# The first modulation chunk is requested between the x tiles, and ten modulation chunks move from the matrix to the vector engine

## The chip, the core and the metric

The kernel runs on one core of one Trainium2 chip. The metric is device time in microseconds (us) for one execution, taken as the median of three runs. In the rows, PE is TensorE's matrix products and PEld its weight loads, DVE is VectorE, ACT is ScalarE, POOL is GpSimd, and SP is the engine whose queue issues most of the loads from HBM.

## The reference

Two transformer blocks over 512 tokens of width 1024, in float32. The change concerns the modulation of the first block: six vectors of 1024 numbers, made by one matrix-vector product with a 1024 x 6144 matrix, which scale and shift the normed input ahead of the mixer (sh1, sc1) and ahead of the feed-forward part (sh2, sc2), and gate what each of the two adds to x (ga1, ga2).

```
c_act = jax.nn.silu(c)
mod = c_act @ ada_w[l] + ada_b[l]
sh1, sc1, ga1, sh2, sc2, ga2 = [m[:, None, :] for m in jnp.split(mod, 6, axis=-1)]
h = rmsnorm(x, pre_mix_g[l]) * (1.0 + sc1) + sh1
y = hybrid_mixer(h, ...)          # GLU projection, causal conv, stick-breaking attention, gates, merge, w_o
x = x + ga1 * rmsnorm(y, post_mix_g[l])
h = rmsnorm(x, pre_ffn_g[l]) * (1.0 + sc2) + sh2
y = swiglu_ffn(h, ...)
x = x + ga2 * rmsnorm(y, post_ffn_g[l])
# second block: retention, latent attention, conv feed-forward, final norm
```

## The kernel before

Every large product is made in three passes of 32-bit "round" numbers (`mm3`, L205 to L207): high part by high part, low by high, high by low. So each weight slab of 128 x 1024 passes through a fixed line: SP loads it into one of two buffers `w_st` (L186), ACT rounds it to `w_hi` (L187), DVE (or POOL) makes the rest `w_lo` (L210), and PE uses both; `w_hi` and `w_lo` have four buffers each. `ORDER` lists the slabs in order of use.

The stages are these. **Start:** the four x tiles (128 tokens each, 512 KB) are loaded, normed by `norm_of` (ACT squares and sums into `junk`, DVE adds a constant, POOL takes the power -0.5, DVE scales), then for each of eight blocks `kb` of 128 features `glu_in(kb)` gets modulation chunk kb, transposes the x tiles into `ps_t` and evacuates them as `hh`, `hf` (ACT) and `hl` (POOL); six GLU products follow. For kb = 0 the 512 tokens are done in two halves. **Attention:** the convolution taps run on DVE, ACT and POOL under the attention's products. **Merge:** for four pairs p, gates, the two branches' outputs and their sum. **wo and boundary:** the product with w_o, the residual, the next norm. **fin and fout:** the feed-forward part. Then the second block.

A modulation chunk (`ada_load`, `ada_acc`) is 1024 x 256 of the matrix: two loads `ad` of 512 KB and eight PE products of 32 columns x 256 (L373) which put four partial sums side by side in `ps_t`, one DVE copy to `acc` (L378), and a product with ones that sums over the partitions: `ada_cols` makes two columns from it (L384, for the scale and shift), `ga_row` a broadcast row (L404, for the gate). Of the 24 chunks eight are used at the start, six during the attention (`AD` sets where), six in the merge (two by `ada_cols`, four by `ga_row(0, ...)`), and four in the fin stage, at m = 4, 8, 12 and 16 (`fin_extra`).

The order on each engine is set when the program is built: a list scheduler with its own time estimates places the instructions; each engine then runs its list in order, and waits at the head of the list for what is not ready. SP's list is one queue, too: a load that waits for a free buffer holds all loads behind it.

Of the kernel before, what the change touches and what calls it, by code (L numbers as in the profile page):

```python
# [8 lines left out]
F32 = mybir.dt.float32  # L9
# [3 lines left out]
AF = mybir.ActivationFunctionType  # L13
ALU = mybir.AluOpType
# [6 lines left out]
NT = 4  # L21
# [69 lines left out]
AOFF = (0, 512, 896, 1152)  # L91
AGRP = ((0,), (1,), (2, 3))
NST = 2


def build(tc, nc, a):
    stacks = []

    def pool(name, bufs=1, side="left", **kw):
        s = ExitStack()  # L100
        p = s.enter_context(tc.tile_pool(name=name, bufs=bufs, side=side, reuse_waits="tile", **kw))
        stacks.append(s)
        return p, s

    def close(*ss):
        for s in ss:
            s.close()
# [6 lines left out]
    psT, _ = pool("psT", 2, space=PSUM)  # L114
    psP, _ = pool("psP", 4, space=PSUM)
    psC, _ = pool("psC", 2, space=PSUM)
    const, _ = pool("const")
    sm, _ = pool("small", 8)
    ring, _ = pool("ring")
    edge, _ = pool("edge", side="right")  # L120
    edge.tile([128, 96], F32, name="edge")
    hpool, _ = pool("hpool", side="right")

    def pt():
        ps_t = psT.tile([128, 512], F32, tag="t", name="ps_t")
        return ps_t
# [15 lines left out]
    vec = const.tile([128, NVEC], F32)  # L142
# [4 lines left out]
    ones = const.tile([128, 128], F32)  # L147
    mhalf = const.tile([128, 8], F32)
    eps1k = const.tile([128, 1], F32)
    zero = const.tile([128, 1], F32)  # L150
    halfpi = const.tile([128, 1], F32)
    cact = const.tile([128, 8, 32], F32)
    adab1 = const.tile([128, 48], F32)
    modA = const.tile([128, 2, 8], F32)
    modB = const.tile([128, 2, 8], F32)
    an32 = const.tile([128, 16], F32)
# [10 lines left out]
    def vcol(name, i):  # L167
        o = VOFF[name] + i
        return vec[:, o:o + 1]
# [8 lines left out]
    def emit_slab():  # L178
# [3 lines left out]
        n = src.shape[1]  # L182
        w_st = ring.tile([128, 1024], F32, tag="st", bufs=NST, name="w_st")
        w_hi = ring.tile([128, 1024], F32R, tag="hi", bufs=4, name="w_hi")
# [7 lines left out]
    def prefetch(n):  # L192
        while W.nxt < min(len(ORDER), W.got + n):
            emit_slab()
# [33 lines left out]
    def transposes(ps, srcs):  # L228
        for j, s in enumerate(srcs):
            r = s.shape[1]  # L230
            nc.tensor.transpose(out=ps[:r, j * 128:(j + 1) * 128], in_=s, identity=ident)  # L231
# [21 lines left out]
    def norm_of(x_t, jp, xn):  # L253
        r = rstd(sumsq(x_t, jp), None, eps1k)
        nc.vector.tensor_scalar(out=xn, in0=x_t, scalar1=r, scalar2=None, op0=ALU.mult)
# [98 lines left out]

    class ADA:
        pool, tag, bufs, nacc = ring, "st", NST, 1
        loaded = {}

    def ada_load(chunk):
        ads = []  # L360
        for hf in range(2):
            ad = ADA.pool.tile([128, 4, 256], F32, tag=ADA.tag, bufs=ADA.bufs, name="ad")
            nc.sync.dma_start(out=ad, in_=a["ada"][chunk][:, 4 * hf:4 * hf + 4, :])
            ads.append(ad)
        return ads

    def ada_acc(chunk, ap_):

        ads = ADA.loaded.pop(chunk, None) or ada_load(chunk)
        ps = pt()  # L370
        for hf, ad in enumerate(ads):
            for b in range(4):
                nc.tensor.matmul(  # L373
                    out=ps[32 * b:32 * b + 32, 0:256], lhsT=cact[:, 4 * hf + b, :], rhs=ad[:, b, :],
                    start=hf == 0, stop=hf == 1,
                )
        acc = ap_.tile([128, 256], F32, tag="acc", name="acc", bufs=ADA.nacc)
        nc.vector.tensor_copy(acc, ps[:, 0:256])  # L378
        return acc, ps[:, 256:512]

    def ada_cols(i, kb, g_name, ap_):
        acc, ps = ada_acc(8 * i + kb, ap_)
        for s in range(2):
            nc.tensor.matmul(  # L384
                out=ps[:, s:s + 1], lhsT=acc[:, s * 128:(s + 1) * 128], rhs=ones[:, 0:1], start=True, stop=True
            )
        sh, sc = 24 * i + kb, 24 * i + 8 + kb
        nc.vector.tensor_tensor(
            out=modB[:, i, kb:kb + 1], in0=ps[:, 0:1], in1=vcol("ada_b", sh), op=ALU.add
        )  # L390
        nc.vector.scalar_tensor_tensor(
            out=modA[:, i, kb:kb + 1], in0=ps[:, 1:2], scalar=adab1[:, sc:sc + 1], in1=vcol(g_name, kb),
            op0=ALU.add, op1=ALU.mult,
        )

# [18 lines left out]
    nc.vector.memset(eps1k, D * EPS)  # L414
    nc.vector.memset(zero, 0.0)
    nc.vector.memset(halfpi, float(np.float32(np.pi / 2)))

    endp, endp_s = pool("endp")
    cacc = endp.tile([128, 4, S], F32, tag="cacc", bufs=1)
# [4 lines left out]
    adp, adp_s = pool("ada", 2, side="right")  # L424
    xs = xin.tile([128, NT, D], F32)
    pos = const.tile([128, NT], I32)
    ADA.pool, ADA.tag, ADA.bufs, ADA.nacc = adp, "ad", 6, 2
    for tt in range(NT):
        nc.sync.dma_start(out=xs[:, tt, :], in_=a["x"][tt * 128:(tt + 1) * 128, :])
    ADA.loaded[0] = ada_load(0)  # L430
    nc.gpsimd.dma_start(out=cst, in_=a["const"])
    masks = adp.tile([128, 256], F32, tag="masks", name="masks", bufs=1)
# [4 lines left out]
    for _n in ("pre_mix_g", "pre_ffn_g"):  # L437
        _o = VOFF[_n]
        nc.vector.tensor_scalar(
            out=vec[:, _o:_o + 8], in0=vec[:, _o:_o + 8], scalar1=32.0, scalar2=None, op0=ALU.mult  # L440
        )
    _o = VOFF["ada_b"]
    nc.vector.tensor_scalar(out=adab1, in0=vec[:, _o:_o + 48], scalar1=1.0, scalar2=None, op0=ALU.add)
    nc.vector.tensor_copy(identb, ident)
    nc.vector.tensor_copy(strictb, masks[:, 0:128])
    nc.vector.tensor_copy(causalb, masks[:, 128:256])
    _o = VOFF["attn_norm_w_2"]
    nc.vector.tensor_scalar(out=an32, in0=vec[:, _o:_o + 16], scalar1=32.0, scalar2=None, op0=ALU.mult)
    _o = VOFF["mla_q_norm_w_2"]
    nc.vector.tensor_scalar(  # L450
        out=lat[:, 0:2], in0=vec[:, _o:_o + 2], scalar1=float(np.float32(16.0 * 96.0 ** -0.5)), scalar2=None,
        op0=ALU.mult,
    )
    nc.vector.tensor_scalar(
        out=lat[:, 2:3], in0=vec[:, _o + 2:_o + 3], scalar1=float(np.float32(np.sqrt(128.0))), scalar2=None,
        op0=ALU.mult,
    )

    for tt in range(NT):
        norm_of(xs[:, tt, :], adp, xs[:, tt, :])  # L460


    glu_ps = [pp() for _ in range(6)]

    def glu_in(kb, halves=1):
        ada_cols(0, kb, "pre_mix_g", adp)
        n = S // halves
        for i in range(halves):
            ps = pt()
            tts = range(i * NT // halves, (i + 1) * NT // halves)  # L470
            transposes(ps, [xs[:, tt, kb * 128:(kb + 1) * 128] for tt in tts])
            evac_h(ps[:, :n], kb, i * n, n, modA[:, 0, kb:kb + 1], modB[:, 0, kb:kb + 1], adp, True)

    glu_in(0, 2)
    for kb in range(KB):
        wh, wl = slab(("glu", kb))
        if kb < KB - 1:
# [2 lines left out]
        for t0 in range(0, S, n):  # L480
            for j in range(6):
# [3 lines left out]
                )  # L485
    ADA.pool, ADA.tag, ADA.bufs, ADA.nacc = ring, "st", NST, 1
    close(adp_s, xin_s)
# [312 lines left out]
    split_o(3)  # L800
    mtmp, mt_s = pool("mtmp", 4)
    grow_p, _gs = pool("growp", side="right")
    ADA.pool, ADA.tag, ADA.bufs = mtmp, "ad", 2
    grow1 = grow_p.tile([128, D], F32)
    for p in range(4):
        if p >= 2:
# [17 lines left out]
        for q in ((0,), (1, 2), (3,), ())[p]:  # L824
            ga_row(0, grow1, accp, q, mtmp)
    ADA.pool, ADA.tag, ADA.bufs = ring, "st", NST
    close(mt_s, endp_s)
# [161 lines left out]
    for tt, banks in gemm_tok([("c2", i) for i in range(4)], h_operand, 416, 4, seg=2):  # L989
        b = banks[tt, 0]  # L990
# [20 lines left out]
    for kb in range(3):  # L1011
        ps = pt()
        transposes(ps, [cT[:, tt, kb * 128:(kb + 1) * 128] for tt in range(NT)])
        sc = lat[:, kb:kb + 1]
        nc.scalar.activation(out=cTh[:, kb, :], in_=ps, func=AF.Identity, scale=sc)
        nc.vector.scalar_tensor_tensor(
            out=cTl[:, kb, :], in0=ps, scalar=sc, in1=cTh[:, kb, :].bitcast(F32), op0=ALU.mult, op1=ALU.subtract
# [218 lines left out]
    for b in range(2):  # L1236
        _, o = halves_of(b)
# [185 lines left out]
```

## Time and profile before

| | |
|---|---|
| median of 3 runs | 1425.65 us (1425.45 to 1426.05) |
| the profiled execution | 1426.3 us, span 1424.6 us |
| PE busy | 1378.3 us (97% of the span) |
| DVE busy | 731.9 us (51%) |
| ACT busy | 582.1 us (41%) |
| POOL busy | 325.1 us (23%) |
| mean granted TensorE clock | 0.991 |

The span runs from the first to the last instruction; the 1.7 us around it belong to the execution and not to the program's instructions. Busy shares are means over stages: what a stage is worth has to be read in that stage.

### The profile page before, as it was taken

The numbers are of one execution on the slowest core, as the hardware profiler recorded it, in microseconds if no ns is written. First come the engines' busy times: TensorE is split into PE (matmuls) and PEld (weight loads), VectorE is DVE, ScalarE is ACT, GpSimd is POOL, SyncE is SP. The second block draws the span as 40 slices with busy tenths as digits, with TensorE's granted clock in tenths as the row PEclk, the third lists the DMA queues.
The fourth block names the chain that finished last, engine by engine and source line by source line (L and its number), as shares of the span: only waits on it lengthen the run. The fifth ranks groups of instructions, "written<-read, shape, count | busy, mean of one in ns | idle before, by whom it ended". The sixth has DMA issues, their size and how long they took to land. (4 is left out here: it accounts for less than half of the span.)

```text
span 1424.6 us, 17617 instructions
## 1 busy us (share of the span) xinstructions
PE 1378.3 (97%) x6846; PEld 1119.7 (79%) x6846; DVE 731.9 (51%) x1132; ACT 582.1 (41%) x953; POOL 325.1 (23%) x329
## 2 busy tenths in 40 slices
PE   6999999999989999999999899999999999999998
PEld 4786777877878888888887788787888888888886
DVE  3299868254365332232333754688256655554334
ACT  4457655322244222222223525668345333333222
POOL 2189745321150000000002533377220000000000
PEclk9998999999999999999999999999999999999999
DMA  9422133564323344333232322001233323232321
GB/s 332 139 83 81 58 103 108 170 201 146 133 68 118 126 126 132 112 104 104 89 104 79 126 95 89 30 16 60 83 110 104 101 92 104 89 104 89 104 90 73
DMA packets 44324, 152.20 MB, mean 107 GB/s; under 512 B 4881, under 2 KB 7057, under 8 KB 44241
## 3 DMA queue, kind: packets, MB, share of 16 engines
q1 hardware_dynamic: 42720, 145.90, 31.0%
q0 software_dynamic: 1376, 4.97, 0.9%
q8 instruction: 54, 0.88, 0.3%
q14 instruction: 30, 0.24, 0.1%
q10 hardware_dynamic: 144, 0.21, 0.0%
HBM read 146.86 MB, written 4.19 MB: 106 GB/s over the span
## 5 line engine op out<-in xcount | busy, mean ns | idle before, releaser
L187 ACT CAST w_hi<-w_st 128x1024 fp32r<-128x1024 f32 (+2 forms) x217 | 225.3, 1039 | 395.6 <-PE ps_p L206 125.9
L210 DVE TENSOR_TENSOR w_lo<-w_st,w_hi 128x1024 fp32r<-128x1024 f32 (+2 forms) x179 | 222.4, 1244 | 258.5 <-ACT w_hi L187 256.6
L205 PE MATMUL ps_p<-hh,w_hi 128*128 128x512 f32 (+1 forms) x740 | 278.0, 382 | 1.9 <-ACT hh L266 1.2
L206 PE MATMUL ps_p<-hl,w_hi 128*128 128x512 f32 (+1 forms) x740 | 279.1, 378 | 0.4 <-POOL hl L210 0.4
L207 PE MATMUL ps_p<-hh,w_lo 128*128 128x512 f32 (+1 forms) x740 | 277.9, 376 | 1.4 <-DVE w_lo L210 1.4
L242 POOL TENSOR_TENSOR r<-q,mhalf 128x1 f32<-128x1 f32 x36 | 21.4, 595 | 768.4 <-DVE q L238 723.9
L205 PEld LDWEIGHTS ps_p<-hh,w_hi 128*128 128x128 f32 x740 | 139.4, 190 | 30.8 <-ACT hh L266 2.5
L207 PEld LDWEIGHTS ps_p<-hh,w_lo 128*128 128x128 f32 x740 | 140.4, 190 | 27.7 <-DVE w_lo L210 2.5
L206 PEld LDWEIGHTS ps_p<-hl,w_hi 128*128 128x128 f32 x740 | 140.6, 190 | 26.0 <-POOL hl L210 1.6
L205 PE MATMUL ps_c<-hh,w_hi 128*128 128x512 f32 (+1 forms) x354 | 130.4, 368 | 3.1 <-ACT hh L266 2.0
L206 PE MATMUL ps_c<-hl,w_hi 128*128 128x512 f32 (+1 forms) x354 | 130.0, 368 | 1.1 <-POOL hl L210 1.1
L207 PE MATMUL ps_c<-hh,w_lo 128*128 128x512 f32 (+1 forms) x354 | 128.6, 363 | 0.0
L210 POOL TENSOR_TENSOR w_lo<-w_st,w_hi 128x1024 fp32r<-128x1024 f32 (+1 forms) x38 | 93.1, 2455 | 67.0 <-ACT w_hi L187 47.1
L210 DVE TENSOR_TENSOR gl<-gf,gh 128x512 fp32r<-128x512 f32 x44 | 30.4, 690 | 105.6 <-ACT gh L869 105.5
L869 ACT CAST gh<-gf 128x512 fp32r<-128x512 f32 x44 | 27.4, 622 | 135.1 <-PE ps_p L206 124.1
L205 PEld LDWEIGHTS ps_c<-hh,w_hi 128*128 128x128 f32 x354 | 67.3, 190 | 15.9 <-ACT hh L266 2.5
L206 PEld LDWEIGHTS ps_c<-hl,w_hi 128*128 128x128 f32 x354 | 66.9, 189 | 11.7 <-POOL hl L210 1.3
L207 PEld LDWEIGHTS ps_c<-hh,w_lo 128*128 128x128 f32 x354 | 67.1, 189 | 11.0 <-issue 0.8
L207 PE MATMUL ps_p<-w_hi,gl 128*128 128x512 f32 x176 | 68.5, 389 | 0.0
L206 PE MATMUL ps_p<-w_lo,gh 128*128 128x512 f32 x176 | 68.5, 389 | 0.0
L205 PE MATMUL ps_p<-w_hi,gh 128*128 128x512 f32 x176 | 68.5, 389 | 0.0
L510 DVE SCALAR_TENSOR_TENSOR ps_c<-upad,vec,ps_c 128x512 f32<-128x512 f32 x87 | 60.6, 747 | 0.7
(423 smaller groups left out, 2536.0 us busy)
## 6 DMA issues: line engine op xcount, KB each, us to landing
ad<-in_ada SPq DMA_DIRECT2D x48, 512.0 KB, 4.0
w_st<-in_w_fin SPq DMA_DIRECT2D x44, 512.0 KB, 3.7
w_st<-in_w_up SPq DMA_DIRECT2D x44, 512.0 KB, 3.7
w_st<-in_w_win SPq DMA_DIRECT2D x22, 512.0 KB, 3.7
w_st<-in_w_fout SPq DMA_DIRECT2D x22, 512.0 KB, 3.6
w_st<-in_w_down SPq DMA_DIRECT2D x22, 512.0 KB, 3.7
w_st<-in_w_gate SPq DMA_DIRECT2D x16, 512.0 KB, 3.7
w_st<-in_w_wo SPq DMA_DIRECT2D x16, 512.0 KB, 3.7
```

Source lines behind the costliest of these rows:

```text
L187: nc.scalar.copy(w_hi[:, :n], w_st[:, :n])
L205: nc.tensor.matmul(out=out, lhsT=lh, rhs=rh, start=start, stop=False)
L206: nc.tensor.matmul(out=out, lhsT=lh, rhs=rl, start=False, stop=False)
L207: nc.tensor.matmul(out=out, lhsT=ll, rhs=rh, start=False, stop=stop)
L210: (eng or nc.vector).tensor_tensor(out=out, in0=src, in1=hi.bitcast(F32), op=ALU.subtract)
L242: nc.gpsimd.tensor_tensor(out=r, in0=q, in1=mhalf[:, 0:1], op=ALU.pow)
L510: nc.vector.scalar_tensor_tensor(out=out, in0=src, scalar=w, in1=acc, op0=ALU.mult, op1=ALU.add)
L869: nc.scalar.copy(gh, gf[:, k, :])
```

## The change

The change has four parts. (1) The start: only x tiles 0 and 1 are requested ahead of modulation chunk 0; then comes the first GLU slab (`prefetch(1)`), and only then x tiles 2 and 3, which are normed between the two halves of `glu_in(0)`. (2) A one-element silu at the very start makes ACT load the silu table first. (3) Twelve products of the ones tile by itself are put at the head of PE's list; nothing reads them. (4) From the merge on (`ADA.vector = True`, never reset, so in the fin stage too) a chunk's eight partial products are made on DVE: one multiplication and seven multiply-adds over 128 x 256, in place of eight PE products and the copy. The `1 + bias` table is made in place. No result differs but for the order of summation.

```
+    warm = sm.tile([128, 1], F32, tag="q", name="warm")
+    nc.scalar.activation(out=warm, in_=zero, func=AF.Silu)
+    idle = pt()
+    for _ in range(WARM):                                  # WARM = 12
+        nc.tensor.matmul(out=idle[:, 0:128], lhsT=ones, rhs=ones, start=True, stop=True)
...
-    for tt in range(NT):
-        nc.sync.dma_start(out=xs[:, tt, :], in_=a["x"][tt * 128:(tt + 1) * 128, :])
+    def load_x(tts):
+        for tt in tts:
+            nc.sync.dma_start(out=xs[:, tt, :], in_=a["x"][tt * 128:(tt + 1) * 128, :])
+
+    load_x((0, 1))
     ADA.loaded[0] = ada_load(0)
...
-    for tt in range(NT):
-        norm_of(xs[:, tt, :], adp, xs[:, tt, :])
...
-    def glu_in(kb, halves=1):
+    def glu_in(kb, halves=1, late=()):
         ada_cols(0, kb, "pre_mix_g", adp)
         n = S // halves
         for i in range(halves):
+            if i:
+                for tt in late:
+                    norm_of(xs[:, tt, :], adp, xs[:, tt, :])
...
-    glu_in(0, 2)
+    for tt in (0, 1):
+        norm_of(xs[:, tt, :], adp, xs[:, tt, :])
+    prefetch(1)
+    load_x((2, 3))
+    glu_in(0, 2, (2, 3))
...
     def ada_acc(chunk, ap_):
         ads = ADA.loaded.pop(chunk, None) or ada_load(chunk)
+        if ADA.vector:
+            acc = ap_.tile([128, 256], F32, tag="acc", name="acc", bufs=ADA.nacc)
+            for hf, ad in enumerate(ads):
+                for b in range(4):
+                    cc = cact[:, 4 * hf + b, 0:1]
+                    if hf == 0 and b == 0:
+                        nc.vector.tensor_scalar(out=acc, in0=ad[:, b, :], scalar1=cc, scalar2=None, op0=ALU.mult)
+                    else:
+                        nc.vector.scalar_tensor_tensor(
+                            out=acc, in0=ad[:, b, :], scalar=cc, in1=acc, op0=ALU.mult, op1=ALU.add
+                        )
+            return acc, pt()[:, 256:512]
...
-    ADA.pool, ADA.tag, ADA.bufs = mtmp, "ad", 2
+    ADA.pool, ADA.tag, ADA.bufs, ADA.vector = mtmp, "ad", 2, True
```

The list of ACT at the start shows what a late x tile stands behind; `-` is before, `+` is the change, `junk,ss` is the square sum of one x tile, `cact` the silu of c, and `w_hi` the rounding of a GLU slab.

```order
 L250 ACTIVATE junk,ss<-xs 128x1024
-L436 ACT_TABLE_LOAD
-L436 ACTIVATE cact<-vec 128x8
-L250 ACTIVATE junk,ss<-xs 128x1024 x3
-L187 CAST w_hi<-w_st 128x768 x2
+L459 ACTIVATE cact<-vec 128x8
+L250 ACTIVATE junk,ss<-xs 128x1024
+L187 CAST w_hi<-w_st 128x768
 L266 ACTIVATE hh<-ps_t,modB,modA 128x256
 L269 ACTIVATE hf<-ps_t,modB,modA 128x256
+L250 ACTIVATE junk,ss<-xs 128x1024 x2
+L187 CAST w_hi<-w_st 128x768
```

The table load between the first two square sums is gone; the square sums of x tiles 2 and 3, and the second slab's rounding, move behind the first half's `hh` and `hf`. On DVE the part that follows reads so in the changed kernel, from modulation chunk 0 on (`acc` to `modA`), with the two late tiles' `q` and `xs` between the slabs' `w_lo`:

```order
L393 COPY acc<-ps_t 128x256
L403 TENSOR_TENSOR modB<-ps_t,vec 128x1
L406 SCALAR_TENSOR_TENSOR modA<-ps_t,vec 128x1
L210 TENSOR_TENSOR w_lo<-w_st,w_hi 128x768
L236 TENSOR_TENSOR q<-ss,eps1k 128x1
L255 TENSOR_SCALAR xs<-xs,r 128x1024
L236 TENSOR_TENSOR q<-ss,eps1k 128x1
L210 TENSOR_TENSOR w_lo<-w_st,w_hi 128x768
L255 TENSOR_SCALAR xs<-xs,r 128x1024
```

Before, all four tiles' `q` and `xs` stood ahead of `acc`; now the last tile's scaling stands behind the second slab's `w_lo`, which itself needs ACT's rounding of that slab.

In the merge, DVE's list before has one copy for a chunk between the slabs' `w_lo`, the products with the gates (`gat`) and the merged operand's low part (`ml_`):

```order
L817 TENSOR_TENSOR gat<-gat,ps_c 128x512
L210 TENSOR_TENSOR ml__2669<-st,mh 128x512
L378 COPY acc<-ps_t 128x256
L210 TENSOR_TENSOR w_lo<-w_st,w_hi 128x1024
L210 TENSOR_TENSOR ml__2669<-st,mh 128x512
```

The changed list there, from the first of the merge's chunks on:

```order
L379 TENSOR_SCALAR acc<-ad,cact 128x256
L381 SCALAR_TENSOR_TENSOR acc<-ad,cact,acc 128x256 x7
L210 TENSOR_TENSOR w_lo<-w_st,w_hi 128x1024
L775 TENSOR_TENSOR st<-st,ps_c 128x512
L775 TENSOR_TENSOR st<-st,ps_p 128x512
L210 TENSOR_TENSOR w_lo<-w_st,w_hi 128x1024
```

A chunk is now eight instructions ahead of a `w_lo`; later chunks are cut into pieces of one to four between the other work. Behind the merge, at the boundary, ACT's list before, from the square sums of token tile 1's product on:

```order
L250 ACTIVATE junk,ss<-ps_c 128x512
L250 ACTIVATE junk,ss<-ps_p 128x512
L250 ACTIVATE junk,ss<-x_3168 128x1024
L187 CAST w_hi<-w_st 128x1024
L250 ACTIVATE junk,ss<-ps_p 128x512
```

and in the changed kernel:

```order
L250 ACTIVATE junk,ss<-ps_c 128x512
L250 ACTIVATE junk,ss<-ps_p 128x512
L187 CAST w_hi<-w_st 128x1024 x2
L250 ACTIVATE junk,ss<-x_3177 128x1024
L250 ACTIVATE junk,ss<-ps_p 128x512
```

Two slabs' roundings now stand ahead of the square sum of the new x of tile 1.

## Rows read from the trace of the kernel before

**Rows 1.** Stages: us, busy us (count) of PE, PEld, DVE, ACT, POOL, clock, DMA, GB/s.

```profile
11.89:14.03 2.14, 2.14 (x18) 0.69 (x18) 1.06 (x3) 0.00 (x1) 0.54 (x1) 1.00 1.03 416
287.00:362.00 75.00, 75.00 (x389) 55.32 (x388) 36.71 (x52) 18.60 (x24) 11.52 (x8) 1.00 0.53 177
399.00:431.00 32.00, 27.33 (x201) 24.90 (x200) 21.18 (x33) 15.58 (x31) 18.11 (x22) 0.95 0.24 75
431.00:600.00 169.00, 168.17 (x794) 136.39 (x793) 61.07 (x86) 47.70 (x58) 0.19 (x1) 1.00 0.38 123
```

**Rows 2.** PE's longest wait: us in total, times, longest us.

```profile
PE ps_t L373 <- DMA ad<-in_ada: 11.9, 1, 11.9
```

**Rows 3.** Timeline of PE at the start: start us, length us, instruction.

```profile
13.52 1.08 PE L373 MATMUL ps_t<-ad,cact 128*32 128x256 f32 x8
...
17.20 0.80 PE L205 MATMUL ps_p<-hh,w_hi 128*128 128x256 f32 x2
17.79 0.41 PE L205 MATMUL ps_c<-hh,w_hi 128*128 128x256 f32 x1
18.00 0.63 PE L205 MATMUL ps_p<-hh,w_hi 128*128 128x256 f32 x2
...
20.09 0.28 PE L207 MATMUL ps_p<-hh,w_lo 128*128 128x256 f32 x1
20.21 0.28 PE L206 MATMUL ps_p<-hl,w_hi 128*128 128x256 f32 x1
...
26.28 0.73 PE L205 MATMUL ps_p<-hh,w_hi 128*128 128x512 f32 x2
```

**Rows 4.** Timeline of ACT, DVE and POOL at the start.

```profile
9.99 1.06 ACT L250 ACTIVATE junk<-xs 128x1024 bf16<-128x1024 f32 x1
...
12.86 0.75 DVE L255 TENSOR_SCALAR xs<-xs,r 128x1024 f32<-128x1024 f32 x1 [0.66 <-POOL r L242]
...
14.03 1.81 ACT L187 CAST w_hi<-w_st 128x768 fp32r<-128x768 f32 x2 [2.89 <-DMA w_st<-in_w_glu]
...
15.01 0.95 DVE L210 TENSOR_TENSOR w_lo<-w_st,w_hi 128x768 fp32r<-128x768 f32 x1
...
17.04 0.56 ACT L269 ACTIVATE hf<-ps_t,modB,modA 128x256 f32<-128x256 f32 x1
...
17.68 0.73 POOL L210 TENSOR_TENSOR hl<-hf,hh 128x256 fp32r<-128x256 f32 x1 [4.85 <-ACT hf L269]
```

**Rows 5.** Timeline of PE in the merge, around half a chunk.

```profile
323.92 0.40 PE L205 MATMUL ps_p<-oh,w_hi 128*128 128x512 f32 x1
...
325.38 0.40 PE L205 MATMUL ps_p<-oh,w_hi 128*128 128x512 f32 x1
...
326.07 0.39 PE L205 MATMUL ps_p<-oh,w_hi 128*128 128x512 f32 x1
```

**Rows 6.** Timeline of PE in the fin stage, around a whole chunk.

```profile
501.97 0.39 PE L207 MATMUL ps_c<-hh,w_lo 128*128 128x512 f32 x1
...
503.29 0.50 PE L205 MATMUL ps_p<-hh,w_hi 128*128 128x512 f32 x1
```

**Rows 7.** Groups of DVE in the merge, by line and shape: busy, mean ns, idle before.

```profile
L210 DVE TENSOR_TENSOR w_lo<-w_st,w_hi 128x1024 fp32r<-128x1024 f32 x11 | 15.6, 1415 | 6.6 <-ACT w_hi L187 6.5
...
L406 DVE SCALAR_TENSOR_TENSOR grow<-grow,gr 128x256 f32<-128x256 f32 x4 | 1.7, 420 | 0.0
```

**Rows 8.** Timeline of DVE: one `w_lo` beside POOL, three chained multiply-adds.

```profile
331.39 2.27 DVE L210 TENSOR_TENSOR w_lo<-w_st,w_hi 128x1024 fp32r<-128x1024 f32 x1 [0.17 <-ACT w_hi L187]
...
452.46 0.94 DVE L909 SCALAR_TENSOR_TENSOR angles<-angles 128x128 f32<-128x128 f32 x3
```

**Rows 9.** DMA issues in the merge: count, KB each, median us to landing.

```profile
w_st<-in_w_gate SPq DMA_DIRECT2D x3, 512.0 KB, 5.4
```

**Rows 10.** Timeline of ACT and DVE at the boundary.

```profile
397.94 1.04 ACT L187 CAST w_hi<-w_st 128x1024 fp32r<-128x1024 f32 x1
...
399.56 2.35 DVE L210 TENSOR_TENSOR w_lo<-w_st,w_hi 128x1024 fp32r<-128x1024 f32 x2
```

More of the change, by code (lines that the diff above doesn't have):

```diff
@@ L93 @@
 NST = 2
+WARM = 12
 def build(tc, nc, a):
@@ L120, in build @@
     edge, _ = pool("edge", side="right")
-    edge.tile([128, 96], F32, name="edge")
+    edge.tile([128, 16], F32, name="edge")
     hpool, _ = pool("hpool", side="right")
@@ L152, in build @@
     cact = const.tile([128, 8, 32], F32)
-    adab1 = const.tile([128, 48], F32)
     modA = const.tile([128, 2, 8], F32)
@@ L356, in build @@
         pool, tag, bufs, nacc = ring, "st", NST, 1
-        loaded = {}
+        loaded, vector = {}, False
     def ada_load(chunk):
@@ L391, in ada_cols @@
         nc.vector.scalar_tensor_tensor(
-            out=modA[:, i, kb:kb + 1], in0=ps[:, 1:2], scalar=adab1[:, sc:sc + 1], in1=vcol(g_name, kb),
+            out=modA[:, i, kb:kb + 1], in0=ps[:, 1:2], scalar=vcol("ada_b", sc), in1=vcol(g_name, kb),
             op0=ALU.add, op1=ALU.mult,
@@ L442, in build @@
     _o = VOFF["ada_b"]
-    nc.vector.tensor_scalar(out=adab1, in0=vec[:, _o:_o + 48], scalar1=1.0, scalar2=None, op0=ALU.add)
+    for _i in (_o + 8, _o + 32):
+        nc.vector.tensor_scalar(
+            out=vec[:, _i:_i + 8], in0=vec[:, _i:_i + 8], scalar1=1.0, scalar2=None, op0=ALU.add
+        )
     nc.vector.tensor_copy(identb, ident)
```

## The prediction

> **What bounds the kernel now.** I read the stages first, then PE's waits, then the places that the change touches. In the merge, 287 to 362 us, PE is busy for all 75.00 us, and in the fin stage, 431 to 600, for 168.17 of 169 [rows 1]: what leaves PE's list there shortens the kernel, as long as nothing new is late. DVE is busy for 36.71 of the merge's 75 us and 61.07 of fin's 169 [rows 1], so it has room for more, on the mean. The boundary between the product with w_o and fin, 399 to 431, is different: PE is idle there for 4.67 of 32 us, and a chain over ACT, DVE and POOL sets the end [rows 1]. At the start PE waits 11.9 us, by far its longest wait, for modulation chunk 0 [rows 2]. The DMA engines are full by then (share 1.03, 416 GB/s, [rows 1]), so the order of the requests sets when that chunk lands.
>
> **The start.** The second half of chunk 0 is used at 13.52, and the first GLU product runs at 17.20, 3.68 us later [rows 3]. Two x tiles of 512 KB no longer lie ahead of the chunk: 1.05 MB at 416 GB/s is 2.5 us, so its second half should be used at about 11.0. The chain of 3.68 us stays, or gets a little shorter: I put the first GLU product at 14.4, 2.8 us earlier. But the second half of the tokens gets later. ACT has the square sums of x tiles 2 and 3 behind the first half's `hf`, which starts 0.16 before and ends 0.40 after that product [rows 3, 4], so at 14.8. Then come, one after the other: two square sums at 1.06 plus about 0.1 each, to 17.1; the second slab's rounding, 0.9 (half of the 1.81 for two), to 18.0; its `w_lo` on DVE, 0.95, to 19.0; the scaling of tile 3 behind it, 0.75, to 19.75 [rows 4]. Transposes and `hh` take about 0.6, as 16.6 to 17.2 before; the products of the second half start at 20.3. Their low part waits for `hf` and for `hl` on POOL (0.73, [rows 4]), to 21.5; twelve products at 0.12 (20.09 to 20.21, [rows 3]) make 22.95, and a whole chunk's products about 1.0 (1.09 in fin, worked out below), so that block 1 starts at 24.0, not at 26.28 [rows 3]: **-2.3 us**. From there on the blocks follow each other on PE as before. The bounds: nothing is gained if the late tiles take all of it (0 us), and the 2.8 us of the first half plus what a faster clock gives (next paragraph) make 4 us at most.
>
> The table load that goes was on ACT ahead of tile 1's square sum, under the wait for the chunk: nothing. The twelve idle products lie in the same wait of 11.9 us [rows 2]. No row shows one of them; by the nearest, a 128-column transposing product, they take a few us. If they took more than the 9.4 us to the new landing (11.9 - 2.5) they would delay the chunk, which they should not: the trace counts two passes for a float32 product (x8 for the four of half a chunk, [rows 3]), and 24 passes of 128 columns, each at the slow price of 256 (0.21, from 17.79 to 18.00, [rows 3]), are 5.0 us. What they may give is the clock. [...] At the faster level the chunk's products and the sums over partitions, some 1 us each in the chain, lose up to 0.5 us each; I take none of it, since the late tiles' chain on ACT and DVE sets block 1 anyway.
> [...]
>
> **The chunks that leave PE.** In the merge a half chunk stands between two products: L205 to L205 takes 1.46 us with it (323.92 to 325.38) and 0.69 without (325.38 to 326.07), so it costs 0.77 [rows 5]. In fin a whole chunk in one piece costs 503.29 - 501.97 - 0.23 = 1.09 [rows 6], 0.23 being a third of 0.69. Six chunks go from the merge, one of them in one piece there and five cut in halves: 1.1 + 10 x 0.77 = **-8.8 us**. Four go from fin, all in one piece: 4 x 1.09 = **-4.4 us**. The products with ones that follow a chunk stay.
>
> **What DVE takes on.** A multiply-add of 128 x 256 takes 0.420 us (L406, [rows 7]); chained ones start 0.03 further apart than they are long (three of 128 columns in 0.94, [rows 8]), so eight make at most 8 x 0.45 = 3.6 us. In the merge that is 6 x 3.6 = 21.6 on top of 36.7: 58.3 of the 66.2 that are left of the stage, 88%. In fin it is 14.4 on top of 61.1, of 165: hidden by DVE's idle half. In the merge the cover is thin. The instructions queued behind a chunk on DVE are the slabs' `w_lo`, `gat` and `ml_`; PE waits for `w_lo`. A slab takes 5.4 us from request to landing [rows 9], 1.05 to round, 1.2 to 2.3 for `w_lo` [rows 7, 8], some 8 to 9 us in all; two buffers make one slab per 4 to 4.5 us, and PE uses one up in 24 x 0.23 = 5.5. So each pair of slabs has 2 to 3 us to spare, and a chunk per pair takes 3.6 when it lies wholly ahead of a `w_lo`, as the first one does, and less where it is cut. Bounds: 0, when all of it falls into DVE's idle time, and 6 x 1.6 = 9.6 when no chunk is cut. DVE's list cuts five of six, so I take a value near the lower end, **+1.5 us**.
> [...]
>
> **The boundary.** ACT's list now has two roundings ahead of tile 1's square sum, and DVE two `w_lo` ahead of its norm: 2 x 1.04 = 2.1 us later, with 2.35 more on DVE 4.4 [rows 10], while PE waits for `hh`. On the other side the first slabs are ready earlier, and tile 3's chain, which sets the second half of the tokens, has less ahead of it. Bounds -2 (under half of PE's idle 4.67) and +4.4; I take **+1.0**. The second block's list is also reshuffled in its attention part, with the same work: 0, within 2 us either way.
>
> **The sum,** against the profiled execution: 1426.3 - 2.3 - 8.8 - 4.4 + 1.5 + 1.0 = 1413.3. That execution lay 0.65 above the median of the runs, so the median should come to 1412.6.
>
> **Rivals.** (A) DVE becomes the bound of the merge: each chunk holds a `w_lo` up and the merge keeps its length. Speaking for it: 88% of the stage, and POOL's 11.52 us there [rows 1], beside which a `w_lo` is up to 0.86 us longer (2.27 against 1.415, [rows 7, 8]); if all of POOL's time were added, DVE would need 69.8 us of the 66.2 left. Against it: the cut chunks and the four `w_hi`/`w_lo` pairs. Then the -8.8 and the +1.5 go: 1413.3 + 7.3 - 0.65 = 1420.0.
> (B) The start and the boundary go well: the late tiles are not late (-4 in place of -2.3), no new wait in the merge, the boundary gains 2: 1412.6 - 1.7 - 1.5 - 3.0 = 1406.4.
> (C) Slower: a chunk's first multiplication waits at the head of DVE's list for `ad` to land, 5.4 us after a request that SP may itself hold back, and everything behind it waits too. With ten chunks the gain of 15.5 is gone from 1.55 us of PE's time each; the full 5.4 each would give 1426.3 - 15.5 + 54 - 0.65 = 1464, a more likely 2.5 each 1435. Against it: two half-chunk buffers, each free after four instructions, and about 11 us between chunks.
> (D) The change does nothing measurable: the waits of (C) at about 1.5 us each, 1425.
>
> **Chances.** Forecast, 1409 to 1417: 0.58. (A), 1417 to 1422.8: 0.18. (B), 1404 to 1409: 0.14. (D), within 0.2% (2.85 us, about what a measurement of this kernel tells from no change): 0.05. (C): 0.05. So faster 0.90, same 0.05, slower 0.05. The range leaves out (C), (D) and the outer ends of (A) and (B): 1406 to 1420.
>
> **What would show it.** In the changed profile: PE's wait for chunk 0 near 9.4 us; block 1's first product of 512 columns near 24.0; no L373 products behind the attention; DVE busy for about 58 us in a merge some 7 us shorter, and PE's waits for `w_lo` there of 1 to 2 us; fin 4.4 us shorter. The prediction fails if PE waits for `w_lo` or for `mh` in the merge by more than 5 us, if the late x tiles push block 1 to 26 us, or if the boundary's idle time of PE grows past 9 us.

## The result, and the profile after

The changed kernel took 1411.96 us (median of 4 runs, 1410.72 to 1414.83) beside 1425.61 us for the kernel before: a ratio (of the means) of 0.9907, 95% interval 0.9889 to 0.9924. In a second comparison it took 1413.91 us (5 runs, 1410.45 to 1415.90) beside 1425.96 us: 0.9909, 0.9894 to 0.9923. The forecast was 1412.6 us. The sum came out right, in part by luck: most of its terms did not, and errors of both signs cancelled. And a line of the change that is not among its four parts above, and of which the prediction says nothing, turned out to be worth some 14 to 16 us: the unused tile `edge` shrinks from 96 columns to 16.

The stages after. They end earlier than in [rows 1], so their limits are moved with their work (columns as there):

```profile
5.80:10.60 4.80, 0.00 (x0) 0.01 (x1) 1.86 (x8) 1.77 (x5) 1.11 (x2) 0.74 0.98 301
10.60:16.00 5.40, 3.79 (x23) 1.71 (x23) 1.94 (x7) 1.52 (x3) 0.00 (x0) 0.50 1.03 417
289.30:352.20 62.90, 62.90 (x283) 52.10 (x282) 49.70 (x79) 19.78 (x25) 12.38 (x8) 1.00 0.58 186
391.00:424.00 33.00, 25.10 (x180) 22.85 (x179) 19.73 (x32) 15.47 (x31) 16.91 (x22) 0.84 0.26 72
424.00:592.00 168.00, 167.17 (x760) 138.91 (x759) 75.39 (x119) 49.62 (x62) 1.43 (x2) 1.00 0.42 130
```

In the merge (third line) PE is busy all the time, with DVE at 49.70 of 62.90 us. In the boundary (fourth line) PE is idle for 7.90 of 33 us; before it was 4.67 of 32 [rows 1]. PE's longest waits after, up to 430 us (us in total, times, longest):

```profile
PE ps_t L388 <- DMA ad<-in_ada: 4.9, 1, 4.9
PE ps_t L231 <- DVE xn L255: 3.3, 1, 3.3
PE ps_c L205 <- ACT hh L266: 3.3, 1, 3.3
```

The same two of the boundary before (399 to 431):

```profile
PE ps_c L205 <- ACT hh L266: 2.0, 2, 1.4
...
PE ps_t L231 <- DVE xn L255: 0.3, 1, 0.3
```

The wait for chunk 0 fell from 11.9 us [rows 2] to 4.9, but only because the idle products fill 1.11 to 5.75: the chunk is there at 10.62, not at 11.89. In the boundary two waits have grown, the one for `xn` from 0.3 us to 3.3 and the one for `hh` from 2.0 to 3.3. None is in the merge.

To see where the time went I took, for each kernel run, the start of the same instruction at six places in its PE and ACT timelines (block 1's first product, the merge's first with `oh`, the last product with w_o, a product of fin 40 us behind the boundary, fout's first, the last scaling of an output tile) and subtracted the kernel before. Each row is the change within one stretch, from one profiled execution of each kernel; "again" is the changed kernel's second execution, the other columns are experiments told below.

| stretch | predicted | after | again | start_only | chunks_only | idle0 | hold1_edge8 | best |
|---|---|---|---|---|---|---|---|---|
| to block 1's first product | -2.3 | +0.38 | -0.01 | -0.09 | +1.50 | -0.78 | +0.40 | -1.36 |
| from there to the merge | 0 | +1.89 | +1.39 | +0.78 | -0.56 | -0.64 | +0.03 | -1.28 |
| merge and product with w_o | -7.3 | -9.91 | -9.91 | -0.05 | -9.88 | -9.91 | -9.99 | -9.99 |
| boundary | +1.0 | +3.55 | +3.38 | 0.0 | +3.4 | +3.3 | +2.3 | +2.4 |
| fin | -4.4 | -5.09 | -5.09 | 0.0 | -5.1 | -5.1 | -5.2 | -5.2 |
| fout and second block | 0 | -2.28 | -1.02 | -0.04 | -2.59 | -3.85 | -2.19 | -3.74 |
| sum | -13.0 | -11.5 | -11.3 | +0.6 | -13.2 | -17.0 | -14.6 | -19.1 |

Both profiled executions of the changed kernel were among its longest (1414.8 and 1415.1 us), so its -11.5 and -11.3 stand for a typical -12 to -13.7. In the columns shown, the rows of the merge and of fin repeat within 0.2 us wherever the chunks are on VectorE.

**The start.** PE's timeline after, to be held against [rows 3]:

```profile
1.11 4.64 PE L436 MATMUL ps_t<-ones 128*128 128x128 f32 x24 [1.11 <-DVE zero L430]
10.62 1.08 PE L388 MATMUL ps_t<-ad,cact 128*32 128x256 f32 x8 [4.88 <-DMA ad<-in_ada]
...
12.26 1.08 PE L388 MATMUL ps_t<-ad,cact 128*32 128x256 f32 x8
...
15.93 0.80 PE L205 MATMUL ps_p<-hh,w_hi 128*128 128x256 f32 x2 [1.03 <-ACT hh L266]
...
20.28 1.08 PE L388 MATMUL ps_t<-ad,cact 128*32 128x256 f32 x8
...
22.43 0.50 PE L205 MATMUL ps_p<-hh,w_hi 128*128 128x256 f32 x2
...
26.66 0.73 PE L205 MATMUL ps_p<-hh,w_hi 128*128 128x512 f32 x2
```

The first GLU product comes 1.27 us earlier than before, block 1 comes 0.38 later. The late x tiles' chain on ACT and DVE lies between:

```profile
17.40 1.06 ACT L250 ACTIVATE junk<-xs 128x1024 bf16<-128x1024 f32 x1
...
18.45 0.82 ACT L187 CAST w_hi<-w_st 128x768 fp32r<-128x768 f32 x1
21.81 0.56 ACT L266 ACTIVATE hh<-ps_t,modB,modA 128x256 fp32r<-128x256 f32 x1 [2.54 <-PE ps_t L231]
```

```profile
19.30 0.96 DVE L210 TENSOR_TENSOR w_lo<-w_st,w_hi 128x768 fp32r<-128x768 f32 x1 [0.27 <-ACT w_hi L187]
20.18 0.74 DVE L255 TENSOR_SCALAR xs<-xs,r 128x1024 f32<-128x1024 f32 x1
```

**The boundary.** Here ACT, DVE and PE after, around tile 1 (before: [rows 10]):

```profile
389.56 2.00 ACT L187 CAST w_hi<-w_st 128x1024 fp32r<-128x1024 f32 x2 [2.33 <-PE ps_p L207]
391.47 1.05 ACT L250 ACTIVATE junk<-x 128x1024 bf16<-128x1024 f32 x1
...
397.55 1.04 ACT L187 CAST w_hi<-w_st 128x1024 fp32r<-128x1024 f32 x1 [3.50 <-DMA w_st<-in_w_fin]
398.50 1.02 ACT L266 ACTIVATE hh<-ps_t,modB,modA 128x256 fp32r<-128x256 f32 x2
```

```profile
390.65 2.92 DVE L210 TENSOR_TENSOR w_lo<-w_st,w_hi 128x1024 fp32r<-128x1024 f32 x2 [0.46 <-ACT w_hi L187]
...
394.31 0.75 DVE L255 TENSOR_SCALAR xn<-x,r 128x1024 f32<-128x1024 f32 x1 [0.66 <-POOL r L242]
```

```profile
395.11 0.69 PE L231 MATMUL ps_t<-cst,xn 128*128 128x128 f32 x2 [3.31 <-DVE xn L255]
399.11 0.58 PE L205 MATMUL ps_c<-hh,w_hi 128*128 128x256 f32 x1 [3.31 <-ACT hh L266]
```

The transposes that feed `hh` start at 395.11, and ACT is free by then, but the next instruction on its list is the rounding of the third fin slab, whose load lands only at 397.55. `hh` stands behind it until 398.50, and PE waits. The two roundings that the prediction feared, at 389.56, cost the square sum 0.1 us (POOL has tile 1's x ready at 391.4); the `w_lo` pair behind them holds tile 1's norm 0.9 us up (its square sum is read out at 392.6, the norm starts at 393.5).

That is 0.9 of the 3.0 us by which the wait for `xn` grew. The other 2.0 come from PE's own list. POOL's addition that completes tile 1's x, and PE's last product with w_o, before and then after:

```profile
395.19 1.66 POOL L337 TENSOR_TENSOR x<-x,y 128x512 f32<-128x512 f32 x1 [1.52 <-DVE y L334]
...
398.96 0.39 PE L207 MATMUL ps_p<-w_hi,ml__2669 128*128 128x512 f32 x1
```

```profile
389.68 1.68 POOL L337 TENSOR_TENSOR x<-x,y 128x512 f32<-128x512 f32 x1 [1.52 <-DVE y L334]
...
391.32 0.48 PE L207 MATMUL ps_p<-w_hi,ml__2684 128*128 128x512 f32 x1
```

Before, PE still had work with w_o for 2.5 us when tile 1's x was ready; after, for 0.4. Of the products with w_o, 62 stood behind the last one of tile 0 in PE's list before, and 53 stand there now; nine at 0.23 us are 2 us less to cover the norm with. `start_only`, told below, has the 62 and waits 0.3 us, as before; every other kernel with the chunks on VectorE has 53 and waits 3.0 to 3.3, but for `double`, with 41 and 6.3. Beside the longer idle time (7.90 us against 4.67) the clock is low for longer, too: the granted clock reads 0.50 from 393.81 to 404.05 after, with products of 256 columns every 0.21 us and not every 0.12, and before only from 402.28 to 405.69.

### The profile page after: what moved, and what is told of

It is laid out like the page before. It is cut to its first block, busy times and chain, and to the rows that moved or that the text cites. A ratio compares the mean times of both kernels' runs of the same rounds, so it can differ in the third digit from the quotient of the medians.

```text
span 1413.1 us, 17429 instructions
## 1 busy us (share of the span) xinstructions
PE 1370.0 (97%) x6710; PEld 1123.6 (80%) x6710; DVE 764.6 (54%) x1203; ACT 580.4 (41%) x953; POOL 326.1 (23%) x329
## 4 chain that ended last, share of the span: by engine, by line
PE 88%; DVE 4%; ACT 3%; DMA 2%; issue 2%; POOL 1%; SPq 0%; POOLq 0%; ACTq 0%; DVEq 0%
PE ps_p L205 17%; PE ps_p L207 17%; PE ps_p L206 17%; PE ps_c L206 7%; PE ps_c L205 7%; PE ps_c L207 7%; PE ps_t L231 2%; PE ps_t L205 2%; PE ps_t L207 2%; PE ps_t L206 2%; PE ps_t L680 1%; DVE w_lo L210 1%; PE ps_t L388 1%; ACT w_hi L187 1%; DMA ad<-in_ada 1%
```

## The experiments

**The two halves of the change apart.** `start_only` takes the new start and leaves the chunks on PE; `chunks_only` is the kernel before with the ten chunks on VectorE.

```diff
-    ADA.pool, ADA.tag, ADA.bufs, ADA.vector = mtmp, "ad", 2, True
+    ADA.pool, ADA.tag, ADA.bufs = mtmp, "ad", 2          # start_only
```

> The new start alone; all chunks behind the attention stay on PE as before. Theory 1 (the changed kernel's trace: block 1 starts at 26.66 there and not at 24.0, so the start gives nothing): block 1's first 512-column product near 26.7, and the time 1425.6 plus 0.4 to 2.2 us, 1426 to 1428. Theory 2 (the prediction's -2.3, hidden in the changed kernel by something else): block 1 near 24, and 1423.3. The boundary's order on ACT is the one of the kernel before here, so both expect PE idle some 4.7 us there, not 7.9.

Measured: 1427.77 us (11 runs, 1425.94 to 1428.53) beside 1426.00, ratio 1.0008, interval 0.9999 to 1.0017. Block 1 starts at 26.19. Theory 1 holds, and the boundary, with ACT's order there as in the kernel before, keeps its length.

> The kernel before with only the ten chunks of merge and fin on VectorE. Theory 1 (merge -10.0, boundary +3.7, fin -5.1, all three caused by the chunks; the second block's attention -3.0 comes with any new order of the lists or not): 1425.6 - 11.4 = 1414.2, or 1411.2 where the second block gains too; PE idle in the boundary about 7.9 us, with a rounding that waits for its load ahead of tile 1's hh on ACT. Theory 2 (the prediction's terms without the start, -10.7): 1414.9, PE idle in the boundary under 6 us, and the rest of the changed kernel's gain from the start.

Measured: 1412.47 us (4 runs, 1411.67 to 1413.14), ratio 0.9904, 0.9890 to 0.9917. PE waits 3.3 us for `xn` and 3.1 for `hh` in the boundary. So the whole gain is the chunks', and so are the boundary's loss and the gain in the second block, where `start_only` has -0.04.

**The idle products and the clock.** `idle0` has `WARM = 0`, `idle30` has `WARM = 30`. These two share one order of the lists in the attention, which is not the changed kernel's.

> The changed kernel without its idle products. Theory 1 (their effect on the clock is lost in the 4.9 us of waiting for chunk 0): first GLU product at 15.9, 256-column products every 0.21 us until about 21.7, block 1 at 26.7, time within 1 us of the changed kernel's 1412.0. Theory 2 (they bring the faster clock forward): the products stay at 0.21 us longer, block 1 later than 27.2, time 1413 or more. Theory 3 (their clock history makes the slow stretch longer, since the kernel before has products every 0.12 us from 20.1 on): faster products from about 20, block 1 at 25.5, 1411 or less.

> The changed kernel with 30 idle products instead of 12, so that PE is busy until close to the landing of chunk 0 at 10.6. Theory 1 (the clock falls because PE idles from 5.75 to 10.62): the later idle products take about 0.2 us each in place of 0.39, all end by 10.5, the chunk's halves take 0.6 in place of 1.08 and the GLU products start every 0.12 us from the first; block 1 near 24 to 25, the time 1.5 to 2.5 us below the changed kernel's. Theory 2 (no such effect: all 30 at 0.39): they end at 12.7, 2.1 us after the landing, block 1 near 28.7, and the time 2 us above.

Measured: `idle0` 1409.69 us (1409.19 to 1411.40), ratio 0.9887, 0.9873 to 0.9900; `idle30` 1410.76 us (1409.77 to 1411.66), 0.9894, 0.9879 to 0.9909. PE's start in `idle30`:

```profile
10.63 0.64 PE L388 MATMUL ps_t<-ad,cact 128*32 128x256 f32 x8 [0.17 <-DMA ad<-in_ada]
11.82 0.64 PE L388 MATMUL ps_t<-ad,cact 128*32 128x256 f32 x8 [0.55 <-DMA ad<-in_ada]
...
13.01 0.61 PE L399 MATMUL ps_t<-ones,acc 128*128 128x1 f32 x4 [0.18 <-DVE acc L393]
15.77 0.50 PE L205 MATMUL ps_p<-hh,w_hi 128*128 128x256 f32 x2 [2.16 <-ACT hh L266]
```

With PE busy until the landing, half a chunk takes 0.64 us, not 1.08, and the sums 0.61, not 1.01. In the changed kernel's own trace half a chunk takes 1.08 us at 10.62 and 20.28, where the granted clock reads 0.50, and 0.64 at 21.70, beside its step to 1.00 (1.00 from 21.75 to 22.40). So by its times `idle30` had the faster of these two levels at the landing. After 12 products and a pause of 4.9 us it was not; the granted clock reads 0.50 from 10.60 to 16.00. So theory 1 of `idle30` holds for the idle products, which end at 10.46, and for the chunk. Yet the first GLU product starts at 15.77 and not at 15.93, since `hh` comes late: DVE's list has `w_lo` of the first slab, which lands at 12.7, ahead of `modA` (13.63 to 14.57), and ACT's has the square sum of tile 2 ahead of `hh` (14.12 to 15.17). Behind the 2.16 us of waiting for `hh` the faster level goes again: the granted clock reads 0.50 from 16.39 to 19.80, and the low part's products of 256 columns start every 0.21 us. So block 1 starts at 25.87, not at 24 to 25, and the time is 1.2 us below the changed kernel's, not 1.5 to 2.5.

`idle0` comes out at theory 3's numbers, with block 1 at 25.50. Whether for theory 3's reason isn't shown: from which moment the 256-column products start every 0.12 us rather than every 0.21 differs from execution to execution. It is 19.99 us in the kernel before and 19.08 to 22.75 in four others without idle products; it is 21.75 and 20.84 in the two of the changed kernel and 18.82 to 21.93 in six others with twelve. So nothing shows that the twelve help, or that they harm. Why the kernels with 0 and 30 are 1 to 4 us faster stays open in part. `idle0`'s trace gains 0.8 to 1.2 us on those of the changed kernel at the start, 2.0 to 2.5 from block 1 to the merge and 1.6 to 2.8 behind fin, and part of it is time at the low clock, which lies elsewhere in every execution; the idle products' own share can't be told from that.

**The changed kernel again.**

> The changed kernel once more, unaltered, for a second trace beside the next three on one chip. Its profiled execution was the longest of four (1414.8 against a median of 1412.0). Theory 1 (the part ahead of the merge differs from execution to execution, since DMA landings and the clock do): time 1412 within 1.5, merge, boundary and fin as before within 0.3 us (-10.0, +3.7, -5.1 against the kernel before), the difference all ahead of 290 us. Theory 2 (the stages behind differ too): merge, boundary or fin off by more than 1 us.

Measured: as told above. Theory 1 holds for merge, boundary and fin. It fails for the second block, which gained 1.02 in place of 2.28 us; the low clock (granted 0.50) lasts from 911.72 to 921.96 us there, and from 912.63 to 919.46 in the first trace.

**Where DVE's room ends.** `double` does each chained multiply-add in the merge twice.

```diff
+                        if ap_ is endp:
+                            nc.vector.scalar_tensor_tensor(
+                                out=idle2, in0=ad[:, b, :], scalar=cc, in1=acc, op0=ALU.mult, op1=ALU.add
+                            )
```

> The changed kernel with every chained multiply-add of the merge's six chunks done twice, the second into a row that nothing reads: 7 x 0.52 = 3.6 us more of DVE for a chunk. Theory 1 (DVE was 79% busy in the merge, 49.7 of 62.9 us, so it becomes the bound at about 1.8 times the chunk work): five chunks give 49.7 + 18 = 68 of 63 us, PE waits for w_lo or ml_ by 5 us or more, time 1417 or above. Theory 2 (the lists cut the chunks so finely that PE never waits; the sixth chunk and the product with w_o give room): under 2 us, 1412 to 1414.

Measured: 1423.51 us (11 runs, 1421.94 to 1425.84), ratio 0.9983, 0.9974 to 0.9991. The windows of merge and w_o, and PE's longest waits there:

```profile
289.00:352.00 63.00, 63.00 (x283) 52.18 (x282) 57.68 (x94) 18.14 (x23) 11.64 (x8) 1.00 0.53 163
352.00:391.00 39.00, 31.24 (x128) 25.40 (x127) 19.53 (x36) 4.11 (x4) 0.00 (x0) 0.87 0.47 156
```

```profile
PE ps_t L424 <- DVE acc L382: 7.8, 1, 7.8
PE ps_t L231 <- DVE xn L255: 6.3, 1, 6.3
```

The time is theory 1's, the place is neither's. At 92% of the merge DVE still holds nothing of PE's up. What comes late is the last chunk itself, whose sum stands in PE's list under the product with w_o. DVE itself stands still for 4.26 us from 358.6, ahead of that chunk, waiting for PE's sum of the chunk before. The limit is when the chunk is due, not DVE's share of the stage.

**The stall in the boundary.** `hold1` lets the third and fourth fin slab be rounded only after block 1's `hh`, by a bias of zero made from it:

```diff
+        if key in HOLD:                     # ("fin", 1), ("fin", NF + 1)
+            nc.scalar.activation(out=w_hi[:, :n], in_=w_st[:, :n], func=AF.Identity, bias=W.zero)
...
+    W.zero = sm.tile([128, 1], F32, tag="hold", name="hold", bufs=1)
+    nc.vector.tensor_scalar(
+        out=W.zero, in0=hh[:, 1, 0:1].bitcast(F32), scalar1=0.0, scalar2=None, op0=ALU.mult
+    )
```

> The changed kernel, in which ACT's rounding of the third and fourth fin slab gets a bias of zero worked out from hh of block 1, so that it can't stand ahead of tile 1's first hh. Theory 1 (PE's wait of 3.3 us for hh in the boundary is ACT standing at a rounding whose slab lands at 397.6): hh follows its transposes by some 0.5 us, PE's wait shrinks from 3.3 to about 1, and the time falls by 1.5 to 2.5 us, to about 1410. Theory 2 (tile 2 and 3's chain sets the end of the boundary anyway): the wait moves behind it, and the time stays at 1412 within 0.7.

Measured: 1430.46 us (7 runs, 1428.47 to 1430.88), ratio 1.0029, 1.0018 to 1.0040: 16.5 to 18.5 us slower than the changed kernel, which neither theory allows. Beside the changed kernel merge and w_o lost 2.3 us, fin 5.9, fout and the second block 8.3, without a new wait: in fin and in the second feed-forward part sixty products took 14.0 us in place of 13.6. What the edit had changed for them was only a place in memory: the new one-column tile lies ahead of the slab buffers and moves them 32 bytes, while `hh` lies on the other side of the memory, behind the unused tile `edge`. That gave three kernels with nothing but places altered.

```diff
-    edge.tile([128, 16], F32, name="edge")
+    edge.tile([128, 8], F32, name="edge")       # edge8, and hold1_edge8 on top of hold1
+    edge.tile([128, 96], F32, name="edge")      # edge96
```

> The changed kernel with 8 columns in place of 16 in the unused tile edge at the start of the right-hand memory side, so that hh, hl and the other right-hand tiles lie 32 bytes further on; every engine's list of instructions is word for word that of the changed kernel. Theory 1 (hold1 was slow because its one new column moved the slab buffers 32 bytes against hh, and a product whose two operands lie so takes 0.233 us in place of 0.227): products of fin and up 14.0 us per 60, not 13.6, as in hold1; 88 slabs of 24 products there give 2112 / 60 x 0.4 = 14 us, some more in the attention and the merge, the time 1426 to 1431. Theory 2 (hold1 was slow from its two altered roundings): no difference, 1412 to 1414.

> The changed kernel with edge at 96 columns, as in the kernel before, so without that line of the change; the lists are again unaltered, and the right-hand tiles lie 320 bytes lower. Against the slab buffers they are then 64 bytes off modulo 128, and even modulo 64. Theory 1 (the pair of addresses counts modulo 128): slow products as in edge8, and 1426 or more, so that this line of the change was needed. Theory 2 (it counts modulo 64): 13.6 us per 60 products and 1412 to 1414, the line does nothing for the time.

> hold1 (third and fourth fin slab rounded only after the first hh) with edge at 8 columns, which moves hh 32 bytes as the new column moved the slab buffers; the lists are those of hold1. Theory 1 (the stall in the boundary is ACT at a rounding whose slab has not landed, and hold1's loss was its addresses): 1430 falls to the changed kernel's 1412 to 1414 less 1.5 to 2.5, so 1410 to 1412, PE's waits for hh in the boundary 1 us or less in place of 3.3. Theory 2 (tile 3's chain sets the end anyway): 1412 to 1414.

Measured: `edge8` 1431.66 us (1430.27 to 1434.55), ratio 1.0038, 1.0026 to 1.0051; `edge96` 1428.26 us (1427.01 to 1429.70), 1.0012, 1.0003 to 1.0021; `hold1_edge8` 1410.06 us (1409.44 to 1411.77), 0.9888, 0.9874 to 0.9901. The same 30 us of fin in the changed kernel, and then in `edge8`:

```profile
480.00:510.00 30.00, 30.00 (x134) 24.80 (x133) 13.09 (x19) 7.90 (x9) 0.00 (x0) 1.00 0.43 134
```

```profile
480.00:510.00 30.00, 30.00 (x130) 24.19 (x129) 13.72 (x20) 7.74 (x10) 0.00 (x0) 1.00 0.43 131
```

PE is busy throughout in both, at the same clock (1.00), and gets through 130 products and not 134. In the changed kernel they start 0.227 us apart, in `edge8` 0.233:

```profile
506.14 0.39 PE L205 MATMUL ps_p<-hh,w_hi 128*128 128x512 f32 x1
506.37 0.39 PE L206 MATMUL ps_p<-hl,w_hi 128*128 128x512 f32 x1
506.60 0.39 PE L207 MATMUL ps_p<-hh,w_lo 128*128 128x512 f32 x1
```

```profile
505.63 0.39 PE L205 MATMUL ps_p<-hh,w_hi 128*128 128x512 f32 x1
505.86 0.40 PE L206 MATMUL ps_p<-hl,w_hi 128*128 128x512 f32 x1
506.10 0.39 PE L207 MATMUL ps_p<-hh,w_lo 128*128 128x512 f32 x1
```

Theory 1 holds for both edges against theory 2, with `edge8` just above its range. `edge96` moves `hh` by 192 bytes against the slabs as they lay in the kernel before, and rules out a period of 64 bytes; whether the period is 128 these runs don't settle, since the fast kernels lie at 0 and at 512 bytes only. `hold1_edge8`, with the lists of `hold1`, is 20.4 us faster than it, and 2 to 4 us faster than the changed kernel. PE's waits in its boundary:

```profile
PE ps_t L235 <- DVE xn L259: 3.3, 1, 3.3
PE ps_t L235 <- DVE hf L275: 1.6, 2, 0.9
PE ps_c L210 <- POOL hl L214: 1.3, 2, 0.9
PE ps_c L209 <- ACT hh L270: 0.5, 1, 0.5
```

The wait for `hh` is down from 3.3 to 0.5, so it was the rounding that held it. But the waits for `hf` and `hl` grow from 0.9 to 2.9 us and take its place: the boundary is 1.1 to 1.25 us shorter, half of what theory 1 had. The rest of the difference lies ahead of the merge, where it varies between executions: with the same lists as the changed kernel there, the second row of the table has +0.03 in place of +1.89 and +1.39.

**A faster version.** `startvec` is `idle0` with chunks 2, 4 and 6 of the start on VectorE (`ADA.vector = kb in (2, 4, 6)`); `best` adds the held roundings and the 8-column edge.

> The changed kernel without idle products, and with chunks 2, 4 and 6 of the start on VectorE as well. Against the same without them (1409.7): theory 1 (PE is the bound of blocks 1 to 7, and DVE with some 6.6 of 20 us has room for a chunk of 4.1 us in every second block): three times 1.27 us less, 1405.9. Theory 2 (modA and hh come too late, since a chunk's 4.1 us stand in a row on DVE behind its landing): PE waits for hh in these blocks, 1409 to 1412.

> Together: no idle products, chunks 2, 4 and 6 of the start on VectorE (startvec, 1409.0), the two roundings held back, edge at 8 columns. Theory 1 (the held roundings give about 2 us in the boundary): 1407. Theory 2 (nothing from them): 1409 within 0.7.

Measured: `startvec` 1408.96 us (1408.78 to 1410.05), ratio 0.9881, 0.9867 to 0.9894, which can't be told from `idle0`; in its trace 2.1 us are gained ahead of the merge where theory 1 had 3.8, and PE waits 0.9 us for a chunk's sum and 0.4 for `modA`. Some 1.5 of the 2.1 us are lost again in the second block (-2.31 where `idle0` has -3.85), so the time is theory 2's. `best` 1407.18 us (4 runs, 1406.60 to 1407.31), ratio 0.9865, 0.9851 to 0.9878: below both kernels, and theory 1's number.

## Why the prediction came out right

**The start, -2.3: wrong.** It gave nothing (`start_only`). The first step that failed was the landing of chunk 0: "1.05 MB at 416 GB/s is 2.5 us". It came 1.27 us earlier (10.62 against 11.89). The two tiles did free some 3 us, since tiles 2 and 3 took from 6.75 to 9.74 before. But the chunk's first half landed 2.0 us behind the last x tile then, and now lands 3.9 us behind tile 1 (10.49, 6.60). The DMA engines are as busy as before in the 4.8 us up to there (0.98) and move less: 301 GB/s from 5.80 to 10.60, where they moved 351 before, and 289 to 317 in all traces with the new start against 345 to 351 in those without. Why they are slower isn't shown. The chain behind the landing was right: 3.67 us from the second half's use to the first GLU product, 3.68 in [rows 3], of which the forecast had taken 0.3 off. The second step was the late half, put at 20.3: it came at 22.43. Of these 2.1 us, 1.2 are there when tile 3 has been scaled (20.92, forecast 19.75), and they come with the landing; the rest is the late transposes, which stand in PE's list behind half a chunk at the slow level (20.28 to 21.36), so that the products start 1.5 us after the scaling and not 0.6. Block 1 at 26.66 met the condition that the prediction had named for its failure there. The idle products were sized right (5.0 us predicted, 4.64 measured) and gave no more than was put down for them. The up to 0.5 us by which the prediction let the products and the sums get shorter at a faster level, and which it took none of, are 0.44 and 0.40 in `idle30` (1.08 to 0.64, 1.01 to 0.61).

**The chunks off PE, -8.8 and -4.4: right, and too small.** No L373 product is left behind the attention; merge and w_o are 9.91 us shorter, fin 5.09. In fin a chunk cost 1.27, not 1.09: [rows 6] end at the first product behind it, and that one holds PE for 0.34 us and not 0.23 (503.29 to 503.63 in the trace before), the eleven behind it for 2.55 and not 2.49.

**What DVE takes on, +1.5: nothing.** PE had no wait in the merge, so the lower bound, 0, was right, and rivals (A) and (C) fell. A chunk costs 4.4 us of DVE, not 3.6. That DVE is busy for 49.70 us and not for the 58 of the prediction is because the six chunks don't all fall there: of their 48 steps the 62.90 us of the merge have 36, 20.0 us in all, and eight make a chunk.

```profile
L381 DVE SCALAR_TENSOR_TENSOR acc<-ad,cact,acc 128x256 f32<-128x256 f32 x31 | 17.9, 577 | 1.5 <-DMA ad<-in_ada 1.0
...
L379 DVE TENSOR_SCALAR acc<-ad,cact 128x256 f32<-128x256 f32 x5 | 2.1, 422 | 0.0
```

**The boundary, +1.0: mis-sized, within its bounds (+4.4).** It lost 3.4 to 3.55 us, 7.90 us of idle time against the 9 named as failure. The roundings ahead of tile 1's square sum, which the prediction named, cost next to nothing, and the `w_lo` pair behind them, named too, 0.9 us. No term had the other two: PE's own list, which has nine products with w_o less behind tile 0 (2.0 us), and on ACT the third rounding, which waits for its load ahead of `hh`.

**The second block, 0 within 2: mis-sized.** It gained 1.0 to 2.3 us in the changed kernel, 2.6 in `chunks_only` and up to 3.9 in `idle0`. In the kernel before a rounding on ACT stands ahead of a softmax step `sp` (977.32) and waits for PE, and PE then for the step:

```profile
975.17 1.05 ACT L187 CAST w_hi<-w_st 128x1024 fp32r<-128x1024 f32 x1 [1.32 <-PE ps_p L206]
```

```profile
977.83 0.50 PE L205 MATMUL ps_p<-cTh,w_hi 128*128 128x512 f32 x1 [1.28 <-ACT sp L1201]
```

In `chunks_only` that rounding stands elsewhere and the wait is 0.45. All traces with the chunks on VectorE and products of 0.227 us (told below) gain 2.3 to 2.5 us in the stretch that is 933.50 to 1002.11 before, and `start_only`, with the list of before there, gains nothing. PE's waits for `sp` fall in it from 3.8 us to 1.0, with a new one of 0.6 for `xc`. That it is the rounding's place is argued, not shown: no experiment moved it alone. The row's spread comes from ahead of that, 905 to 933 us (+1.65 to -1.17), where the granted clock reads 0.87 to 0.96, from execution to execution.

**What was left out.** "From there on the blocks follow each other on PE as before" failed: from block 1 to the merge the traces of the changed kernel lose 1.4 to 1.9 us, though PE's list there is product for product that of the kernel before. PE waits 0.7 us (0.3 in the second trace) for `hh` at 52 us, where ACT first rounds a slab that lands at 51.1, which is the boundary's pattern again, and 0.4 for `gat` at 149.8. Most of the rest is a stretch at the low clock (granted 0.50), 151.46 to 154.87 us, that the kernel before doesn't have (1.00 there); the same lists in `hold1_edge8` don't have it either, and give +0.03. So this row scatters by up to 1.9 us between executions of the same lists.

What was missing, the start's 2.3 to 2.7, these 1.4 to 1.9 and the boundary's 2.4 to 2.55, was paid for in the most part by merge, fin and the second block, which gave 2.6, 0.7 and 1.0 to 2.3 more than their terms. That the sum lies so near the measured time is luck in that part. That the chunks' gain was left to be seen at all hangs on the line that narrows `edge` by 320 bytes: the change also drops a tile of 192 bytes ahead of the slab buffers, and both together move slabs and `hh` against each other by 512 bytes, at which the products are as fast as before. Without that line (`edge96`) the same lists take 1428.26 us. The prediction costed neither.

## What to carry to other kernels

When a change moves the size of any tile, look at where the operands of the main products then lie; a shift of 32 bytes was worth more here (20.4 us between `hold1` and `hold1_edge8`) than everything else in the change. What a load ahead gives back is not its bytes over the rate of another stretch: here 3.0 us were freed and 1.27 gained. Work that is taken off a busy engine is costed up to where the engine is back in its step; and where it covered a chain on other engines, count what is left in the busy engine's list behind the step on which the chain starts. On an engine with a fixed list, a conversion that waits for a load belongs behind the step on which the busiest engine waits.

## What the runs showed of the hardware

**Two operands' places.** Products of 512 columns with a slab as weights and `hh` or `hl` moving start every 0.227 us when the two tiles lie as in the kernel before, or at 512 bytes from there (the changed kernel, and `hold1_edge8`, which moves both by 32 more). They start every 0.233 us when one of the two is moved so that they lie at 192 (`edge96`), 480 (`hold1`) or 544 bytes (`edge8`). Sixty of them take 13.6 and 14.0 us. In fout, where both operands are on the slabs' side, it stays 13.6 in all of these. Why, and with what period, is not shown.

**DVE beside POOL.** Three chained multiply-adds take 1.52 us alone (312.60) and 2.43 when a POOL addition runs from 302.40 to 303.87:

```profile
302.24 2.43 DVE L381 SCALAR_TENSOR_TENSOR acc<-ad,cact,acc 128x256 f32<-128x256 f32 x3
...
312.60 1.52 DVE L381 SCALAR_TENSOR_TENSOR acc<-ad,cact,acc 128x256 f32<-128x256 f32 x3
```

The first of these takes 0.91 us more, beside 1.47 us of POOL's addition; what makes the difference is not shown. It did not reach PE, which is busy for all 62.90 us of the merge, since DVE had the time (49.70 us busy).
